# First group of a bidirectional recurrence: low-rank products emitted one direction early, the output gate beside the value projection, one addition moved to ScalarE

## The chip, the cores and the metric

One core of one Trainium2 chip runs the whole program in one launch. The metric is device time in microseconds (us) of that launch, median of several runs. The engines are named as the profile names them: PE (TensorE, matmul), PEld (its weight loads), DVE (VectorE), ACT (ScalarE), POOL (GpSimd), SP (SyncE, which issues most DMAs).

## The reference, cut to what matters

A trunk of four layers over 256 context and 256 latent positions of width 1024: a gated mixer, an RWKV-7 layer (bidirectional), an attention layer, and a gated mixer again. The change touches the RWKV-7 layer only. Its features and its recurrence are

```python
decay = exp(-exp(log_w))             # log_w from w0 + tanh(h w_lora1) w_lora2, per direction n
a     = sigmoid(a0 + (h a_lora1) a_lora2)                                     # per direction n
k_dir = k * (1 + (a - 1) * k_a);  kk = k*k_k / |k*k_k|
for t:  S = S*w_t - (S kk_t)(kk_t a_t)^T + v_t k_t^T;   y_t = S r_t           # both directions
out = (norm(y) + bonus(r, k_dir, v)) * silu(z);   z = (lerped h) w_in[3]
```

There are 16 heads of 64, two directions, 512 positions. The kernel works in chunks of 64 positions, so that the recurrence becomes matmuls and the inverse of triangular 64x64 matrices.

## The kernel before, in words

`rwkv` runs, after the projections r, k, kk and the two low-rank factors (`wl`, `al`) are made, four **groups** of four heads. The steps of a group g are:

- `features(g)`: four **lanes** (two pairs of heads `pr` by two directions `n`). A lane takes two second low-rank products on PE (`pw`, `pa`, lines L715 and L716), a tanh of each on ACT (L730, L735), adds 1 to the first (L731, on POOL), runs a prefix sum on DVE (L739), two exponentials on ACT (L741, L742), and forms the tiles `AR` (L752, L753) and `BK` (L767 on POOL, L768 on DVE). Its inputs k, r, kk come back from DRAM (`fetch`, L720), the weights of the products are loaded by L707 and split in two by a cast (L709) and a subtraction (L711).
- `inverse(g)`: the products `nab` (L789) for the four lanes, copied into `X` (L792, L794), a transposition (L801), 31 steps of substitution on DVE (L806, L807), two transpositions back (L811, L813), and a correction of small products (`pg` L826, `px` L837), which ends in `X`.
- `chain(g)`: eight steps of the recurrence (pz, pu, py, pd and, one step ahead, `operands`: pe, pbk). From the second pu on it needs `X` of its group.
- `gate(g)`: 32 matmuls (L976) for z, with its weights and inputs loaded by L964 and L971, a tanh and a product.

`values()` is not split by groups: for each half c of the columns it makes four blocks of v (L1076, eight matmuls each), a reversed copy of each (`prv`, L1083) written out to DRAM (L1091), and transposed copies (`vfm`, L1096). Its weights `wv` are loaded by L1063, two tiles of 1 MB for each half.

The order of the work is written by hand with `interleave`: each flow is a generator that gives up its turn at every `yield`, and the flows take turns by weights. A scheduler then sets the order on every engine from that; every engine works through its own row in order, and SP too issues its loads in order. Before the change, `values()` runs beside `features(0)` and then `inverse(0)`; in group g, `chain(g)` runs beside `features(g+1)`, `inverse(g+1)`, `gate(g)` and the output of the group before.

All small tiles of `features` share one ring `f` of 7 buffers, and `pw` and `pa` share one PSUM buffer (tag `f`). The pool of these tiles ("scan") is opened where the tiles of the projections before it are closed, so a first write to a tile waits for the last use of what lay at that place.

Of the kernel before, what the change touches and what calls it, by code (L numbers as in the profile page):

```python
# [8 lines left out]
F32 = mybir.dt.float32  # L9
# [89 lines left out]
def body(tc, I, out):  # L99
# [389 lines left out]
    def rwkv(m, tail):  # L489
# [182 lines left out]
        nc.gpsimd.memset(cmask[:, :, 0:1], 0.0)  # L672
        Pt = [st(f"P{i}", [128, 8, 65], 1) for i in range(2)]
# [20 lines left out]
        def seg(t):  # L694
            return t.rearrange("p (s t) -> p s t", s=2)
# [4 lines left out]
        def features(g, f):  # L700
            f["12"] = st("12", [128, 4, 8], 3)
            for pr in range(2):
                o = g * 2 + pr
                w2 = {}
                for nm in "wa":
                    raw = st("f", [128, T], NF)[:, 0:256].rearrange("p (n c) -> p n c", n=2)
                    nc.sync.dma_start(out=raw, in_=I[f"rw_{nm}2"][:, :, o * 128:o * 128 + 128])  # L707
                    whi, wlo = st("w2" + nm, [128, 2, 128], 1, F32R), st("l2" + nm, [128, 128], 1, F32R)
# [3 lines left out]
                    w2[nm] = whi, wlo  # L712

                def second(p, nm, n):
# [3 lines left out]
                def fetch(nm, tag="f", n=NF):  # L718
                    t = st(tag, [128, T], n)
                    nc.sync.dma_start(out=t, in_=spill[nm, o])  # L720
                    return t

                ko, ro, kk = fetch("k"), fetch("r"), fetch("kk")
                kd = []
                for n in range(2):
                    lane = n * 2 + pr
                    pw = ps("pw", "f")
                    second(pw, "w", n)
                    tw = st("f", [128, T], NF)
                    S.activation(rev(tw, n), seg(pw), AF.Tanh, scale=0.5, bias=half[:, n, o:o + 1])  # L730
                    nc.gpsimd.tensor_scalar(tw, tw, 1.0, None, ALU.add)  # L731
                    pa = ps("pa", "f")
                    second(pa, "a", n)
                    ta = st("f", [128, T], NF)
                    S.activation(rev(ta, n), seg(pa), AF.Tanh, scale=0.5, bias=half[:, 2 + n, o:o + 1])  # L735
                    yield
                    c = st("f", [128, T], NF)
                    c8 = c.rearrange("p (c t) -> p c t", c=8)
                    V.tensor_tensor_scan(c, cmask.rearrange("p c t -> p (c t)"), tw, 0.0, ALU.mult, ALU.add)  # L739
                    P = Pt[n]  # L740
                    S.activation(P[:, :, 1:65], c8, AF.Exp, scale=-KAPPA2)  # L741
                    S.activation(c, c, AF.Exp, scale=KAPPA2)  # L742
                    nc.gpsimd.tensor_copy(f["12"][:, lane, :], P[:, :, 64])
                    yield

                    def r4(x):

                        return rev(x, n).rearrange("p s (c t) -> p s c t", c=4)

                    for sg in range(2):  # L750
                        ar = st(f"AR{sg}", [128, 4, 2, 64], 8)
                        V.tensor_tensor(ar[:, :, 0, :], r4(kk)[:, sg], P[:, sg * 4:sg * 4 + 4, 0:64], ALU.mult)  # L752
                        V.tensor_tensor(ar[:, :, 1, :], r4(ro)[:, sg], P[:, sg * 4:sg * 4 + 4, 1:65], ALU.mult)  # L753
                        f["AR"][lane, sg] = ar
                    yield
                    b = tw
                    V.scalar_tensor_tensor(out=seg(b), in0=seg(ta), scalar=1.0, in1=rev(kk, n), op0=ALU.add, op1=ALU.mult)
                    S.activation(ta, ta, AF.Identity, scale=half[:, 4, o:o + 1], bias=kab[:, o:o + 1])
                    yield
                    V.tensor_tensor(seg(ta), seg(ta), rev(ko, n), ALU.mult)  # L760
# [716 lines left out]
```

## Time and profile before

| | |
|---|---|
| median of three runs | 1611.43 us (1610.21 to 1616.43) |
| the profiled execution, whole | 1612.92 us |
| its span, first to last instruction | 1611.1 us |
| PE busy | 1519.5 us, 94% of the span |
| DVE / ACT / POOL busy | 1149.1 / 795.2 / 101.1 us |
| mean clock granted to TensorE | 0.98 |
| the stage of the change (end of the projections to the last inverse) | from 543.6 to 935.8 us of the span |

The profiled execution lies 1.5 us above the median. Its span leaves out 1.8 us around the first and the last instruction. Busy time of PE is a share that all stages make up together; the stage of the change is read in windows of its own.

### The profile page before, as it was taken

The page shows a single profiled execution, that of the slowest core. Times are in us where ns is not written, and L with a number is a line of the kernel's source. Part 1 is how long each engine was busy: PE and PEld are TensorE (multiplying, and loading weights), DVE is VectorE, ACT ScalarE, POOL GpSimd, SP SyncE. Part 2 cuts the span into 40 slices and gives each one's busy share as a digit, 9 for nine tenths or more (in the row PEclk, how much of TensorE's full clock was granted, in tenths as well). Part 3 has the DMA queues.
Part 4 walks back from the last instruction along what each step waited for, and adds up shares of the span by engine and source line. Part 5 has one row for each costly group of instructions (what it writes and reads, how often), then busy time and mean ns, then how long its engine had stood idle before and what let it go on. Part 6 is the DMA issues. An engine that isn't in the chain of part 4 may idle for free.

```text
span 1611.1 us, 29355 instructions
## 1 busy us (share of the span) xinstructions
PE 1519.5 (94%) x11860; PEld 1181.4 (73%) x11860; DVE 1149.1 (71%) x2160; ACT 795.2 (49%) x1434; POOL 101.1 (6%) x135
## 2 busy tenths in 40 slices
PE   5999999999988998999998999799999999989998
PEld 2768888888966644776776777688777777768887
DVE  3769998864898377586887844778766666665876
ACT  4534331223665354345345332569866766356543
POOL 0000000000000132303213000000000000000000
PEclk9999999999999999899999999999999999989999
DMA  9766567742144652532433133134321222265452
GB/s 352 271 246 224 191 218 260 261 153 79 53 144 150 183 164 70 153 96 74 126 99 94 62 100 121 53 118 145 115 74 53 80 85 92 70 233 199 165 183 79
DMA packets 95176, 229.07 MB, mean 142 GB/s; under 512 B 26048, under 2 KB 52160, under 8 KB 80576
## 3 DMA queue, kind: packets, MB, share of 16 engines
q1 hardware_dynamic: 92736, 223.00, 40.8%
q10 hardware_dynamic: 2304, 4.20, 0.7%
q8 instruction: 93, 1.52, 0.4%
q14 instruction: 43, 0.35, 0.1%
HBM read 208.81 MB, written 17.83 MB: 141 GB/s over the span
## 4 chain that ended last, share of the span: by engine, by line
PE 47%; DVE 7%; ACT 5%; issue 1%; POOL 1%; DMA 0%; ACTq 0%; POOLq 0%; DVEq 0%
PE fm L323 5%; PE op L323 4%; PE pg L976 3%; PE fm L324 2%; PE op L1047 2%; PE op L324 2%; PE pz L323 2%; PE pu L323 2%; PE po L1358 2%; PE sc L1376 2%; PE pe L862 2%; PE sc L1377 1%; PE pv L416 1%; PE pv L417 1%; PE pz L324 1%
## 5 line engine op out<-in xcount | busy, mean ns | idle before, releaser
L191 DVE TENSOR_TENSOR lo<-raw,hi 128x2048 fp32r<-128x2048 f32 (+3 forms) x161 | 251.7, 1567 | 108.6 <-ACT hi L190 108.1
L190 ACT CAST hi<-raw 128x2048 fp32r<-128x2048 f32 (+3 forms) x161 | 212.1, 1324 | 226.9 <-PE op L327 40.6
L258 DVE SCALAR_TENSOR_TENSOR junk<-adaw,scb 128x1024 f32<-128x1024 f32 x112 | 136.7, 1221 | 10.0 <-DMA adaw<-in_ada_wT 8.1
L323 PE MATMUL op<-s,hi 128*128 128x512 f32 x256 | 91.6, 400 | 0.0
L415 PE MATMUL pv<-hi,hp 128*128 128x512 f32 x192 | 78.2, 409 | 9.1 <-ACT hi L190 6.0
L416 PE MATMUL pv<-lo,hp 128*128 128x512 f32 x192 | 77.7, 405 | 1.7 <-DVE lo L191 1.7
L323 PE MATMUL fm<-hx,hi 128*128 128x512 f32 x200 | 74.1, 411 | 4.1 <-ACT hx L317 3.8
L417 PE MATMUL pv<-hi,hp 128*128 128x512 f32 x192 | 77.2, 402 | 0.0
L324 PE MATMUL op<-s,lo 128*128 128x256 f32 x256 | 71.1, 280 | 0.0
L976 PE MATMUL pg<-xz,wz 128*128 128x256 f32 x256 | 70.2, 408 | 0.0
L767 POOL TENSOR_TENSOR BK<-f 64x256 f32<-64x256 f32 x64 | 57.3, 895 | 44.4 <-DVE f L760 27.4
L866 DVE TENSOR_TENSOR E<-pe,masks 128x512 f32<-128x512 f32 x64 | 41.5, 682 | 25.5 <-PE pe L862 23.0
L324 PE MATMUL fm<-hx,lo 128*128 128x256 f32 x200 | 56.7, 288 | 2.0 <-DVE lo L191 2.0
L323 PEld LDWEIGHTS op<-s,hi 128*128 128x128 f32 x256 | 48.1, 188 | 12.5 <-issue 1.3
L1076 PE MATMUL pv<-wv,xv 128*128 128x512 f32 x128 | 57.2, 596 | 0.0
L1047 PE MATMUL op<-Y,wo 128*128 128x256 f32 x192 | 55.8, 427 | 1.3 <-DVE xT L1051 1.3
L323 PE MATMUL fm<-cq,hi 128*128 128x512 f32 x144 | 55.7, 422 | 0.0
L976 PEld LDWEIGHTS pg<-xz,wz 128*128 128x128 f32 x256 | 47.0, 197 | 11.5 <-issue 3.8
L415 PEld LDWEIGHTS pv<-hi,hp 128*128 128x128 f32 x192 | 37.7, 197 | 19.4 <-ACT hi L190 6.6
L326 PE MATMUL pu<-hp,hi 128*128 128x512 f32 x128 | 51.1, 400 | 0.0
L327 PE MATMUL pu<-hp,hi 128*128 128x512 f32 x128 | 50.5, 395 | 0.0
L328 PE MATMUL pz<-hp,lo 128*128 128x512 f32 x128 | 50.5, 395 | 0.0
(413 smaller groups left out, 4088.2 us busy)
## 6 DMA issues: line engine op xcount, KB each, us to landing
adaw<-in_ada_wT SPq DMA_DIRECT2D x36, 1024.0 KB, 4.9
raw<-in_sgu_v SPq DMA_DIRECT2D x16, 1024.0 KB, 4.8
raw<-in_sgu_u SPq DMA_DIRECT2D x16, 1024.0 KB, 4.8
raw<-in_sgu_z SPq DMA_DIRECT2D x16, 1024.0 KB, 4.7
raw<-in_sgu_o SPq DMA_DIRECT2D x16, 1024.0 KB, 4.8
adaw<-in_ada_w SPq DMA_DIRECT2D x24, 512.0 KB, 9.6
xz<-xz SPq DMA_DIRECT2D x32, 256.0 KB, 4.2
raw<-in_ml_z SPq DMA_DIRECT2D x16, 512.0 KB, 3.6
```

The lines of the kernel that those rows point to most:

```text
L190: S.copy(hi[:, sl], raw[:, sl])
L191: V.tensor_tensor(lo[:, sl], raw[:, sl], hi[:, sl], ALU.subtract)
L258: V.scalar_tensor_tensor(out=junk, in0=raw[:, f, :], scalar=1.0, in1=scb[:, c, :], op0=ALU.mult, op1=ALU.mult, accum_out=m[:, t * 2 + f, c ...
L323: PE.matmul(p, whi, x, start=start, stop=False)
L324: PE.matmul(p[:, 0:256], wlo, x[:, 0], start=False, stop=stop)
L415: PE.matmul(pv[tb], hs[k][:, 0, sl], whi[:, ws_], start=k == 0, stop=False)
L416: PE.matmul(pv[tb], hs[k][:, 0, sl], wlo[:, ws_], start=False, stop=False)
L417: PE.matmul(pv[tb], hs[k][:, 1, sl], whi[:, ws_], start=False, stop=k == 7)
L767: nc.gpsimd.tensor_tensor(bk[H[h], 2 * h:2 * h + 7:2, :], k4[H[h], sg], c4[H[h], sg], ALU.mult)
L976: PE.matmul(p, ws[k // 4][:, k % 4, pr * 128:pr * 128 + 128], xs[k // 2][:, k % 2, :], start=k == 0, stop=k == 7)
L1047: PE.matmul(p[:, ob], w[:, k, ob, :], y[:, k], start=k == 0, stop=k == 1)
L1076: PE.matmul(p, xv[:, k, tb * 128:tb * 128 + 128], ws[k // 4][:, k % 4, :], start=k == 0, stop=k == 7)
```

## The change

1. In group 0 the order of `features` is written out: the products and the tanh of a lane (`front`) are emitted one direction before the rest of that lane (`back`), and the weights of the second pair (`operand(1)`) at the very start. For that the first group borrows tiles: k, r, kk and the prefix sums go into the spare buffers of `X` and `BK`, the second pair's weights into two of `BK`, and `pa` gets the PSUM buffer with tag `n`. `features` of the groups 1 to 3 keep their order.
2. In all groups the addition of 1 moves from POOL to ACT (an Identity with a bias of one).
3. `gate(0)` no longer runs beside `chain(0)`. It follows `values()`, in the flow that runs beside `features(0)` and `inverse(0)`, and takes the tiles of `wv` for its weights and inputs.
4. `values()` gives up its turn once more, in the middle of each block; its ring `v` has 6 buffers where it had 8. Its first 16 turns run beside `features(0)`, the rest and the gate beside `inverse(0)`.

```diff
+            if g == 0:
+                x = st("X", [128, 32, 64], 2)
+                spare = [x[:, 8 * i:8 * i + 8, :] for i in range(4)] + [st("BK0", [128, 9, 64], 8)[:, 0:8, :] for i in range(4)]
+                spare = [t.rearrange("p u t -> p (u t)") for t in spare]
+                wide = [st("BK1", [128, 9, 64], 8, F32R) for i in range(2)]
+            def fetch(nm, o):
+                t = spare.pop(0) if spare else st("f", [128, T], NF)
+                nc.sync.dma_start(out=t, in_=spill[nm, o])
+                return t
...
-                    nc.gpsimd.tensor_scalar(tw, tw, 1.0, None, ALU.add)
-                    pa = ps("pa", "f")
...
+                S.activation(tw, tw, AF.Identity, bias=one)
+                pa = ps("pa", "f" if g else "n")
...
+                ds = [operand(0)]
+                t0 = front(ds[0], 0)
+                ds.append(operand(1))
+                yield
+                t1 = front(ds[0], 1)
+                yield from back(ds[0], 0, *t0)
+                t0 = front(ds[1], 0)
+                yield from back(ds[0], 1, *t1)
+                total(ds[0])
+                t1 = front(ds[1], 1)
+                yield from back(ds[1], 0, *t0)
+                yield from back(ds[1], 1, *t1)
+                total(ds[1])
...
+                w = vw.tile([128, 8, 256], F32, tag="w", name="wz", bufs=3)
+                    x = vw.tile([128, 8, 256], F32, tag="w", name="xz", bufs=3)
...
+                        if k == 3:
+                            yield
-                    v = vw.tile([128, T], F32, tag="v", name="v", bufs=8)
+                    v = vw.tile([128, T], F32, tag="v", name="v", bufs=6)
...
-        interleave((values(), 20), (chained(features(0, fs[0]), inverse(fs[0])), 50))
+        beside = chained(values(), gate(0, fs[0]))
+        interleave((features(0, fs[0]), 18), (islice(beside, 16), 16))
+        interleave((inverse(fs[0]), 25), (beside, 24))
...
-            steps, ahead, z = chain(g, f), iter(()), gate(g, f)
+            steps, ahead, z = chain(g, f), iter(()), gate(g, f) if g else iter(())
```

What this does to the rows of instructions is shown at three places. The first is SP, where the stage's loads begin, with the semaphores that each load waits for in brackets (DMAHW: an earlier DMA; PE_49: a count of finished PE work). Before:

```order
L683 DMA f<-wl 64x512 [waits DMAHW1_49,DVE_49]
L683 DMA f<-wl 64x512 [waits DMAHW2_49]
L683 DMA f<-al 64x512 [waits DMAHW4_49,PE_49,Activation_49]
L683 DMA f<-al 64x512 [waits DMAHW5_49]
L1063 DMA wv<-in_rw_v 128x2048 [waits DMAHW6_49]
L1063 DMA wv<-in_rw_v 128x2048 [waits DMAHW7_49]
L707 DMA f<-in_rw_w 128x2x128 [waits DMAHW0_49]
```

After (L685 is the old L683, L714 the old L720, L1120 the old L1063, L723 the old L707):

```order
L685 DMA f<-wl 64x512 [waits DMAHW2_49]
L714 DMA X<-k_3339 128x512 [waits DMAHW4_49,PE_49]
L714 DMA X<-r_3628 128x512 [waits DMAHW5_49]
L714 DMA X<-kk_3413 128x512 [waits DMAHW6_49]
L685 DMA f<-al 64x512 [waits DMAHW7_49,Activation_49]
L685 DMA f<-al 64x512 [waits DMAHW0_49]
L1120 DMA wv<-in_rw_v 128x2048 [waits DMAHW1_49]
L1120 DMA wv<-in_rw_v 128x2048 [waits DMAHW3_49,DMAHW2_49,Activation_49]
L723 DMA f<-in_rw_w 128x2x128
```

Three loads into the borrowed `X` now stand ahead of `al` and of the values' weights. In the built program the count that the first of them waits for is that of the last product but one of the r projection's last block (pj, L327); the count that `al` waited for before belonged to an earlier block.

The second place is PE, from the last product of the projection (pj) on. Before:

```order
L328 MATMUL pj<-xs,lo 128x512
L1076 MATMUL pv<-wv,xv 128x512 x8
L715 MATMUL pw<-wx,w2w 128x512
L716 MATMUL pw<-wx,l2w 128x512
L1083 MATMUL prv<-v,flip 128x512
L715 MATMUL pa<-ax,w2a 128x512
L716 MATMUL pa<-ax,l2a 128x512
L1076 MATMUL pv<-wv,xv 128x512 x8
```

After (L1133 is the old L1076, L740 and L741 the old L715 and L716):

```order
L1133 MATMUL pv<-wv,xv 128x512 x2
L740 MATMUL pw<-wx,w2w 128x512
L741 MATMUL pw<-wx,l2w 128x512
L740 MATMUL pa<-ax,w2a 128x512
L1133 MATMUL pv<-wv,xv 128x512
L741 MATMUL pa<-ax,l2a 128x512
L1133 MATMUL pv<-wv,xv 128x512
...
L1133 MATMUL pv<-wv,xv 128x512 x4
```

The first lane's products now follow two products of the values, where eight stood ahead of them, and the second lane's products come before the block's last four.

The third place is PE at the end of the first group's inverse. Before:

```order
L1083 MATMUL prv<-v,flip 128x512
L1076 MATMUL pv<-wv,xv 128x512 x8
L826 MATMUL pg<-Dm,X 32x32 x32
L1096 MATMUL vfm<-ident,v 128x128
L1083 MATMUL prv<-v,flip 128x512
L1096 MATMUL vfm<-ident,v 128x128 x3
L715 MATMUL pa<-ax,w2a 128x512
L716 MATMUL pa<-ax,l2a 128x512
L837 MATMUL px<-X,Tm 32x32 x32
```

After (L1033 is the gate, the old L976; L878 and L889 the old L826 and L837):

```order
L1142 MATMUL prv<-v,flip 128x512
L1155 MATMUL vfm<-ident,v 128x128 x2
L1033 MATMUL pg<-xz,wz 128x256 x4
L1155 MATMUL vfm<-ident,v 128x128 x8
L1033 MATMUL pg<-xz,wz 128x256 x20
L878 MATMUL pg<-Dm,X 32x32 x32
L1033 MATMUL pg<-xz,wz 128x256 x4
L889 MATMUL px<-X,Tm 32x32 x32
L1033 MATMUL pg<-xz,wz 128x256 x4
```

Twenty-four of the gate's 32 products now stand between the last block of values and the first small product that needs the inverse, the other eight between the small products.

## Rows read from the trace of the kernel before

**Rows 1.** The page: busy time, share of the span and instructions of each engine.

```profile
PE 1519.5 (94%) x11860; PEld 1181.4 (73%) x11860; DVE 1149.1 (71%) x2160; ACT 795.2 (49%) x1434; POOL 101.1 (6%) x135
```

**Rows 2.** Busy time of each engine by stage: from:to in us from the span's start, length, busy us and instructions of PE, PEld, DVE, ACT, POOL, then the clock granted to TensorE, the share of the DMA engines and GB/s. The bounds are the start of the values, their second half, the start and end of PE's wait for the first inverse, the first product of the recurrence, and then by turns the start and the end of DVE's work on the inverse of groups 1 and 2.

```profile
543.60:583.50 39.90, 39.46 (x111) 16.77 (x109) 21.68 (x41) 21.01 (x35) 16.30 (x19) 1.00 0.58 163
583.50:624.60 41.10, 39.39 (x332) 19.12 (x331) 35.12 (x76) 16.69 (x36) 12.22 (x13) 1.00 0.40 107
624.60:629.80 5.20, 0.00 (x0) 0.00 (x0) 4.79 (x13) 0.57 (x1) 0.00 (x0) 0.90 0.24 50
629.80:656.60 26.80, 24.00 (x410) 18.57 (x410) 12.81 (x20) 14.23 (x25) 6.75 (x9) 0.70 0.56 169
656.60:691.80 35.20, 31.50 (x601) 25.13 (x602) 20.02 (x43) 15.75 (x37) 11.70 (x13) 0.95 0.40 128
691.80:735.10 43.30, 41.67 (x630) 32.18 (x623) 42.23 (x109) 15.87 (x32) 4.32 (x6) 0.99 0.30 93
735.10:792.20 57.10, 51.99 (x928) 38.68 (x926) 37.01 (x78) 32.61 (x64) 19.86 (x22) 0.97 0.33 99
792.20:836.20 44.00, 42.02 (x616) 31.81 (x616) 42.59 (x110) 16.21 (x32) 1.92 (x2) 1.00 0.31 97
```

**Rows 3.** The order of time on PE, at the start of the values and around the first inverse: start us, us, engine line op out<-in, shape, records (an f32 matmul leaves two), and in brackets the idle time before it with what ended it.

```profile
543.37 0.39 PE L328 MATMUL pj<-xs,lo 128*128 128x512 f32 x1
543.60 7.03 PE L1076 MATMUL pv<-wv,xv 128*128 128x512 f32 x16
550.06 0.79 PE L715 MATMUL pw<-wx,w2w 128*128 128x512 f32 x1
...
592.36 1.08 PE L789 MATMUL nab<-AR,BK 64*32 64x64 f32 x64 [1.61 <-ACT X L794]
...
629.84 1.92 PE L826 MATMUL pg<-Dm,X 32*32 32x32 f32 x64 [5.29 <-DVE Dm L811]
631.95 1.91 PE L1083 MATMUL prv<-v,flip 128*128 128x512 f32 x2
...
643.83 0.74 PE L789 MATMUL nab<-AR,BK 64*32 64x64 f32 x34 [1.45 <-ACT X L841]
653.46 3.26 PE L976 MATMUL pg<-xz,wz 128*128 128x256 f32 x8
660.57 1.99 PE L976 MATMUL pg<-xz,wz 128*128 128x256 f32 x8
```

**Rows 4.** Windows of 2 us, columns as in Rows 2, for the clock granted after PE's wait.

```profile
634.00:636.00 2.00, 2.00 (x31) 1.12 (x31) 0.00 (x0) 1.96 (x5) 0.70 (x1) 0.61 0.00 0
654.00:656.00 2.00, 2.00 (x6) 1.60 (x5) 0.44 (x1) 0.00 (x0) 0.00 (x0) 0.50 1.01 242
```

**Rows 5.** SP's queue around the start of the values (start us, us, line, load), and the wait that held the second low-rank factor there (engine line waited for: us in total, times, longest).

```profile
532.72 1.10 SPq L683 DMA_DIRECT2D f<-al  x2
533.88 3.60 SPq L1063 DMA_DIRECT2D wv<-in_rw_v  x2
545.01 0.65 SPq L707 DMA_DIRECT2D f<-in_rw_w  x1
549.30 0.43 SPq L720 DMA_DIRECT2D f<-kk  x1
SPq L683 <- PE pj L327: 3.8, 1, 3.8
```

**Rows 6.** Issues from 530 to 560 us: load, engine, count, KB each, median us from issue to landing; and, last, the shortest, median and longest landing of all four loads of `wv`.

```profile
wv<-in_rw_v SPq DMA_DIRECT2D x3, 1024.0 KB, 7.3
vt<-v SPq DMA_DIRECT2D x4, 64.0 KB, 6.3
f<-in_rw_w SPq DMA_DIRECT2D x1, 128.0 KB, 2.8
DMA to landing us min/median/max: 5.5/6.9/8.4
```

**Rows 7.** The order of time on ACT and DVE: the weights of the first products, and the first and second inverse.

```profile
547.85 0.40 ACT L709 CAST w2w<-f 128x256 fp32r<-128x256 f32 x1
550.22 0.60 DVE L711 TENSOR_TENSOR l2w<-f,w2w 64x128 fp32r<-64x128 f32 x2
596.85 1.95 DVE L801 STREAM_TRANSPOSE Dm<-X 128x1024 f32<-128x1024 f32 x1 [3.92 <-ACT X L792]
629.69 1.87 DVE L813 STREAM_TRANSPOSE X<-Tm 128x1024 f32<-128x1024 f32 x1
691.78 1.94 DVE L801 STREAM_TRANSPOSE Dm<-X 128x1024 f32<-128x1024 f32 x1 [4.70 <-ACT X L792]
```

**Rows 8.** The addition on POOL (duration ns min/median/max, first and last start), and two operations of ACT with one 128x512 f32 input in SBUF (count, busy us, mean ns, idle before).

```profile
L731 POOL TENSOR_SCALAR f<-f x16: 1489/1491/1583, 552.1 to 874.1; 128x512 f32<-128x512 f32 x16
L758 ACT ACTIVATE f<-f,kab,half 128x512 f32<-128x512 f32 x16 | 12.9, 807 | 7.5 <-DVE f L757 7.5
L742 ACT ACTIVATE f<-f 128x512 f32<-128x512 f32 x16 | 10.0, 624 | 0.4
```

**Rows 9.** The order of time on DVE and POOL while an addition of POOL runs beside the steps of the inverse.

```profile
599.84 0.70 DVE L806 TENSOR_TENSOR tmp<-Dm,Tm 128x87 f32<-128x87 f32 x1
600.57 0.25 DVE L807 TENSOR_TENSOR Tm<-Tm,tmp 128x87 f32<-128x87 f32 x1
599.82 1.49 POOL L731 TENSOR_SCALAR f<-f 128x512 f32<-128x512 f32 x1 [7.68 <-issue]
```

More of the change, by code (lines that the diff above doesn't have):

```diff
@@ L701, in features, with operand @@
             f["12"] = st("12", [128, 4, 8], 3)
-            for pr in range(2):
+            spare, wide = [], []
+            if g == 0:
[7 more added lines that the diff above has]
+                return t
+            def operand(pr):
                 o = g * 2 + pr
@@ new lines, in front, with back, r4 @@
+                S.activation(rev(tw, n), seg(pw), AF.Tanh, scale=0.5, bias=half[:, n, o:o + 1])
+                S.activation(tw, tw, AF.Identity, bias=one)
+                pa = ps("pa", "f" if g else "n")
+                second(pa, "a")
+                ta = st("f", [128, T], NF)
+                S.activation(rev(ta, n), seg(pa), AF.Tanh, scale=0.5, bias=half[:, 2 + n, o:o + 1])
+                return tw, ta
+            def back(d, n, tw, ta):
+                o, lane = d["o"], n * 2 + d["pr"]
+                ko, ro, kk = d["k"], d["r"], d["kk"]
+                c = spare.pop(0) if spare else st("f", [128, T], NF)
+                if g == 0:
+                    spare.append(c)
+                c8 = c.rearrange("p (c t) -> p c t", c=8)
+                V.tensor_tensor_scan(c, cmask.rearrange("p c t -> p (c t)"), tw, 0.0, ALU.mult, ALU.add)
+                P = Pt[n]
+                S.activation(P[:, :, 1:65], c8, AF.Exp, scale=-KAPPA2)
+                S.activation(c, c, AF.Exp, scale=KAPPA2)
+                nc.gpsimd.tensor_copy(f["12"][:, lane, :], P[:, :, 64])
+                yield
+                def r4(x):
+                    return rev(x, n).rearrange("p s (c t) -> p s c t", c=4)
+                for sg in range(2):
+                    ar = st(f"AR{sg}", [128, 4, 2, 64], 8)
+                    V.tensor_tensor(ar[:, :, 0, :], r4(kk)[:, sg], P[:, sg * 4:sg * 4 + 4, 0:64], ALU.mult)
+                    V.tensor_tensor(ar[:, :, 1, :], r4(ro)[:, sg], P[:, sg * 4:sg * 4 + 4, 1:65], ALU.mult)
+                    f["AR"][lane, sg] = ar
+                yield
+                b = tw
+                V.scalar_tensor_tensor(out=seg(b), in0=seg(ta), scalar=1.0, in1=rev(kk, n), op0=ALU.add, op1=ALU.mult)
+                S.activation(ta, ta, AF.Identity, scale=half[:, 4, o:o + 1], bias=kab[:, o:o + 1])
+                yield
+                V.tensor_tensor(seg(ta), seg(ta), rev(ko, n), ALU.mult)
+                d["kd"].append(ta)
+                b4, c4, k4 = (x.rearrange("p (s c t) -> p s c t", s=2, c=4) for x in (b, c, ta))
+                for sg in range(2):
+                    bk = st(f"BK{sg}", [128, 9, 64], 8)
+                    for h in range(2):
+                        nc.gpsimd.tensor_tensor(bk[H[h], 2 * h:2 * h + 7:2, :], k4[H[h], sg], c4[H[h], sg], ALU.mult)
+                    V.scalar_tensor_tensor(out=bk[:, 1:8:2, :], in0=b4[:, sg], scalar=-0.5, in1=c4[:, sg], op0=ALU.mult, op1=ALU.mult)
+                    f["BK"][lane, sg] = bk
+                yield
@@ L776, in features @@
+            for pr in range(2):
+                d = operand(pr)
+                for n in range(2):
+                    t = front(d, n)
+                    yield
+                    yield from back(d, n, *t)
+                total(d)
                 yield
```

100 lines of the change are left out of this document (39 added, 61 removed).

## Prediction, made before the changed kernel ran

> **What bounds the kernel now.** The busy times come first: PE works 94% of the span, DVE 71%, ACT 49%, POOL 6% [rows 1]. That is a mean over the program, so the windows of the stage come next [rows 2]. From 543.6 to 624.6 us PE is busy 39.46 of 39.9 and 39.39 of 41.1 us at a granted clock of 1.00: there PE's amount of work is the time. Then PE stands still for 5.2 us, in which DVE is busy 4.79, and in the next 26.8 us the clock averages 0.70. In the group after that the picture splits. While DVE works on an inverse (691.8 to 735.1) both are full, DVE 42.23 and PE 41.67 of 43.3 us. Between two inverses (735.1 to 792.2) PE has 51.99 of 57.1 and DVE 37.01.
>
> The order of time on PE names the gaps [rows 3]: 5.29 us before the first small product `pg`, ended by DVE's `Dm`, and two of 1.61 and 1.45 us before `nab`, ended by ACT's copy into `X`. What the long gap costs behind it stands in the fine windows [rows 4]: PE is busy all 2.00 us of each, yet the granted clock is 0.61 and 0.50, the lower of the two levels (1.2 GHz). Of the 24.0 us of PE work in the 26.8 us window, 30% was lost to that, 7.2 us [rows 2].
>
> So beside 1.6 + 1.45 us of short waits there is one long wait, worth 5.3 + 7.2 us with what follows. Last I read SP's queue, since loads decide when a stage can begin. Before the change, `al` was issued at 532.7 and the first `wv` at 533.9, ten us before their first product, so PE went from the projection's end to `pv` without a gap [rows 3, 5].
>
> **The change part by part.**
>
> *The gate as cover.* PE's row after the last `nab` runs from about 596.9 (where DVE starts the inverse, [rows 7]) to 624.55, 27.7 us, while DVE has `Dm` ready 33 us after its start (629.84 less 596.85, [rows 3, 7]). By the order, three value products less stand in that stretch (7.03 us for eight, so −2.6, [rows 3]), and 24 gate products and twelve small transposed copies more. A gate product is two records; eight records took 3.26 us at the lower clock and 1.99 behind it [rows 3], so 24 products are 12 us; the copies I put at 1. That is 38 us of PE work against 33: the gap goes and with it the fall of the clock. The two short waits go too, as more PE work stands ahead of them: −8.4 us of waits, −7.2 of clock. If the cover failed, both would come back.
>
> The gate's inputs take the places of `wv`, so the first `xz` can be loaded only from the fourth product before the end of the values. Three and a half us of products, one `prv` (1.91 us at the lower clock [rows 3], so about 1) and the copies lie over its issue and landing. Small loads near a 1 MB load landed after 6.3 us in the median, a quiet one after 2.8 [rows 6]: a wait of 0 to 3 us, taken as +1.
>
> *The start.* In the row of SP, loads of k, r and kk into the borrowed `X` now stand ahead of `al` and both `wv`. The first waits for the last products of the projection, which end near 543.5 [rows 3]; before, `al` waited for an earlier block, and only 3.8 us [rows 5]. Everything behind waits with it: three loads at 0.43 and two at 0.55 put the first `wv` at about 546, and it lands 5.5 to 8.4 us later [rows 5, 6], at 551.5 to 554.4, where its first product stood at 543.60. After two products PE meets `pw`, whose weights are issued behind both `wv` (another 3.6 us, [rows 5], so near 549) and need 2.8 to 6.3 us to land and some 1.1 for the cast and the subtraction [rows 6, 7]: 553 to 556.5. So PE idles 8 to 12 us less the 1.8 us of those two products, and runs some of the next 5 us at the lower clock, as after the gap before. This stage was PE's own, so nothing hides it: +8 to +15, taken as +11.
>
> *The turn order.* The fourth `nab` stands behind three value products (2.6) and one `prv` (1.0) more, less the 1.6 us wait that they fill. With the start, the first inverse begins 11 + 3.6 − 1.6 = 13 us late, near 610.
>
> *Where this leaves PE.* To the second inverse: +11 − 8.4 − 7.2 + 1 = −3.6. But half of the gate, 16 products and 8 us, was done after that inverse's start and now comes before it, and two `pw` (0.9) go behind: the second inverse starts at 691.8 + 3.5, about 695. Those 8 us are missing from PE's row afterwards and come back only where PE sets the pace. Of the 100.4 us to the third inverse that is the 57.1 between inverses; in the other 43.3 DVE is as full [rows 2]. I take that share, 57%, so 4.6 come back (bounds 0 and 8). From the third group on, the orders of both kernels differ only in a lane's place. Net without the lanes: −3.6 + 8 − 4.6 = −0.2.
>
> *The addition.* On POOL it takes 1.49 us, sixteen times [rows 8]. For ACT's Identity on the same tile no row exists; the two nearest with one 128x512 input took 0.62 and 0.81 us [rows 8], I take 0.70: 0.8 saved for each lane. The 11 us on ACT lie in an engine that is half idle. In the lane the addition stands between tanh and prefix sum, so it counts where DVE waits for a lane between two inverses, for one or two of four lanes in each of three groups: 3 to 6 times 0.8, taken as −3.6 (0 to −7). POOL beside DVE also costs: a step of the inverse took 0.70 us beside an addition, where the next, of equal size, took 0.25 [rows 9]; 16 times 0.45 is at most 7 us, most of it where DVE isn't waited for, so nothing is added for it.
>
> The Trainium skill ("SBUF — State Buffer", section "Who interferes with whom") says that a DVE instruction with two SBUF inputs and a GpSimd instruction that reads SBUF exclude each other for the whole instruction. By that rule each addition would block DVE for its full 1.49 us. The row doesn't agree in size: the DVE step started 0.02 us after the addition and was done after 0.70, before the addition's end [rows 9].
>
> Sum: −0.2 − 3.6 = −3.8 against the profiled 1612.9 us gives 1609, and the median lies 1.5 lower: **1608 us**. The bounds that matter are the start (−3 to +4), the gate that is paid back (−3.4 to +4.6) and the lanes (−3.4 to +3.6). The likeliest case's own range is 1601 to 1615.
>
> **Rivals.**
>
> *B, faster: PE is the bound throughout.* For it speaks PE's 94%, and its 52 of 57 us between inverses. Then all 8 us of the gate return, the start costs 8, and the lanes are worth 7: 8 − 8.4 − 7.2 + 0 − 7 = −15, so 1612.9 − 15 − 1.5 = 1597. Against it: in each inverse DVE is as full as PE. The case that the borrowed tiles don't hold the loads up belongs here too; then the start costs nothing, but the semaphores in the order speak against it.
>
> *C, slower: the first inverse's delay is carried on.* Each group's inverse, recurrence and next features form one chain; if that sets the pace, the 13 us by which the first inverse is late are not made up by removed PE waits, and only the lanes' 3.6 come off: 1612.9 + 13 − 3.6 − 1.5 = 1621. It decides if the second inverse starts after 700. For it: both engines full in the inverses, and `X` awaited by the second step of the recurrence. Against it: before the change PE had 24 + 31.5 us of work in the 62 us between, part of it at half clock, which makes slack for a late chain.
>
> *D, DVE freed.* If the addition did block DVE for all of its time, 24 us of DVE would go, of which the inverses and lanes could turn perhaps half into time, beside the −3.8: near 1595. The exclusion that the Trainium skill states on the page named above is this case. One row speaks against it.
>
> **How the numbers follow.** Chances: the forecast 0.48, B 0.29, C 0.20, D 0.03. 0.5% or 8 us is about what a measurement of this kernel can tell from no change, so "same" is 1603.4 to 1619.5: B and D are faster, C slower, the forecast the same. The range takes in B's centre with a little for a cheaper start, and C's centre: 1594 to 1622.
>
> **What would show it.** In the trace after: SP's `al` and `wv` issued after 543.5, the first `pv` after 551 and a clock near 0.5 behind it; no wait of PE before the first inverse's small products, and a clock of 1.00 from 620 to 660; inverses starting near 610 and 695; the addition on ACT at about 0.7 us. The prediction falls if PE starts the values without a gap (then B, or better), if the second inverse starts after 700 (C), or if the gate's loads arrive so late that PE waits before the gate and the clock falls there instead.

## The result, and the profile of the changed kernel

The changed kernel takes 1630.68 us (median of four runs, 1624.32 to 1636.55), the kernel before 1612.82 beside it: ratio 1.0108, 95% interval 1.0059 to 1.0158. It is slower by about 18 us, above the range of 1594 to 1622, where the forecast was 3 us shorter than before. The profiled execution took 1626.96 us, 14.0 more than that of before.

Where the 14 us stand is read from the starts of the four inverses on DVE. Before, they are at 596.85, 691.78, 792.22 [rows 2, 7] and 894.92; after, at 609.74, 702.81, 808.92 and 909.52: +12.9, +11.0, +16.7, +14.6. The loss is there before the first inverse starts, and nothing behind it gives it back. In the profiled execution after, the projection ended at 541.9 us where it ended at 543.8 before, so counted from there the first inverse is late by 14.8 us.

The start of the values, SP's queue and then PE after (start us, us, engine line op; in brackets the idle time before it and what ended it):

```profile
541.70 0.33 SPq L714 DMA_DIRECT2D X<-k  x1
542.55 0.42 SPq L714 DMA_DIRECT2D X<-kk  x1
543.07 1.14 SPq L685 DMA_DIRECT2D f<-al  x2
544.25 3.33 SPq L1120 DMA_DIRECT2D wv<-in_rw_v  x2
...
547.63 0.63 SPq L723 DMA_DIRECT2D f<-in_rw_w  x1
```

```profile
551.33 3.35 PE L1133 MATMUL pv<-wv,xv 128*128 128x512 f32 x4 [9.44 <-DMA wv<-in_rw_v]
554.51 0.50 PE L740 MATMUL pw<-wx,w2w 128*128 128x512 f32 x1
...
608.17 1.08 PE L841 MATMUL nab<-AR,BK 64*32 64x64 f32 x64
...
645.97 4.54 PE L1033 MATMUL pg<-xz,wz 128*128 128x256 f32 x12 [2.10 <-DMA xz<-xz]
650.44 1.20 PE L878 MATMUL pg<-Dm,X 32*32 32x32 f32 x64
...
668.98 1.12 PE L971 MATMUL pu<-Z,X 64*64 64x64 f32 x16
```

Before, `al` left at 532.72 and `wv` at 533.88 [rows 5], and the first product of the values stood at 543.60 without a gap [rows 3]. Now `wv` leaves at 544.25 and PE waits 9.44 us for it. The 5.29 us wait for `Dm` [rows 3] is gone: the gate's products run there until 650.44, after a wait of 2.10 us for `xz`.

DVE after, the end of the first inverse and the second:

```profile
609.74 1.96 DVE L853 STREAM_TRANSPOSE Dm<-X 128x1024 f32<-128x1024 f32 x1 [20.94 <-ACT X L844]
639.99 2.09 DVE L863 STREAM_TRANSPOSE Dm<-Tm 128x1024 f32<-128x1024 f32 x1
702.81 1.94 DVE L853 STREAM_TRANSPOSE Dm<-X 128x1024 f32<-128x1024 f32 x1 [2.84 <-ACT X L844]
750.32 1.87 DVE L865 STREAM_TRANSPOSE X<-Tm 128x1024 f32<-128x1024 f32 x1
```

`Dm` is ready at 642.08, so the small products start 8.4 us after they could. And DVE stood idle for 20.94 us ahead of the first inverse: the features, started 4.5 us later than before, were done early on DVE, and then `nab` waited in PE's row behind products of the values.

The stages after, in windows as in [rows 2]: the gap, what follows it, the first inverse, what follows the wait for `xz`, from the first inverse's end to the second, the second inverse, to the third, the third.

```profile
541.80:551.30 9.50, 0.09 (x1) 0.00 (x1) 2.75 (x4) 4.18 (x7) 0.00 (x0) 0.61 0.93 308
551.00:555.00 4.00, 3.67 (x6) 1.43 (x6) 0.52 (x3) 0.76 (x2) 0.00 (x0) 0.61 1.03 387
609.74:643.89 34.15, 34.12 (x110) 18.94 (x108) 32.29 (x74) 11.39 (x20) 4.58 (x5) 1.00 0.48 124
646.00:650.00 4.00, 4.00 (x11) 3.20 (x12) 0.75 (x2) 0.69 (x3) 0.97 (x2) 0.57 0.17 60
643.89:702.81 58.92, 49.52 (x978) 40.94 (x982) 31.25 (x64) 28.88 (x60) 15.47 (x19) 0.87 0.41 128
702.81:752.19 49.38, 46.86 (x688) 36.49 (x684) 46.81 (x118) 18.52 (x37) 3.19 (x5) 0.92 0.16 50
752.19:808.92 56.73, 52.18 (x882) 37.65 (x880) 34.80 (x71) 32.54 (x63) 14.85 (x19) 0.88 0.31 94
808.92:849.95 41.03, 39.06 (x554) 30.08 (x548) 38.69 (x98) 13.30 (x27) 0.00 (x0) 1.00 0.32 98
```

For the stretch between the first two inverses the row of before that answers is:

```profile
631.56:691.78 60.22, 53.76 (x954) 41.96 (x952) 31.05 (x61) 29.96 (x62) 18.43 (x22) 0.85 0.48 150
```

Beside the first inverse PE now works 34.12 of 34.15 us at a clock of 1.00, as forecast. Right behind it the wait for `xz` is followed by a clock of 0.57, from 646 to 650: the prediction named a wait before the gate with a fall of the clock there as a sign that it falls. From its end to the second inverse the length hardly changes (58.92 and 60.22), though PE has less to do: its idle time grew from 6.5 to 9.4 us and the clock is still 0.87. Of the 9.4 us, 2.1 are the wait for `xz`, and 5.4 are three waits for the recurrence's `S` and `UV`. The second inverse grew from 43.3 to 49.4 us, with 118 instructions of DVE in it for 109 [rows 2] (among the added ones three of `E`, one of `UV` and two of `Y`, all of the recurrence, and three of the output, `xT`); the third shrank from 44.0 to 41.0.

### The profile page after: what moved, and what is told of

Its sections match the earlier page's. It is cut to its first block, busy times and chain, and to the rows that moved or that the text cites. A ratio compares the mean times of both kernels' runs of the same rounds, so it can differ in the third digit from the quotient of the medians.

```text
span 1625.2 us, 29332 instructions
## 1 busy us (share of the span) xinstructions
PE 1528.9 (94%) x11860; PEld 1191.0 (73%) x11860; DVE 1155.1 (71%) x2160; ACT 804.5 (50%) x1450; POOL 79.0 (5%) x120
## 5 line engine op out<-in xcount | busy, mean ns | idle before, releaser
L417 PE MATMUL pv<-hi,hp 128*128 128x512 f32 x192 | 76.8, 400 | 0.0
L1033 PE MATMUL pg<-xz,wz 128*128 128x256 f32 x256 | 67.8, 401 | 2.1 <-DMA xz<-xz 2.1
L1133 PE MATMUL pv<-wv,xv 128*128 128x512 f32 x128 | 59.2, 609 | 9.4 <-DMA wv<-in_rw_v 9.4
L1033 PEld LDWEIGHTS pg<-xz,wz 128*128 128x128 f32 x256 | 46.7, 194 | 12.5 <-issue 2.6
L1133 PEld LDWEIGHTS pv<-wv,xv 128*128 128x128 f32 x128 | 24.2, 194 | 38.0 <-issue 37.4
L327 PE MATMUL pu<-hp,hi 128*128 128x512 f32 x128 | 50.5, 395 | 0.0
```

The source lines that it names most:

```text
L417: PE.matmul(pv[tb], hs[k][:, 1, sl], whi[:, ws_], start=False, stop=k == 7)
L1033: PE.matmul(p, ws[k // 4][:, k % 4, pr * 128:pr * 128 + 128], xs[k // 2][:, k % 2, :], start=k == 0, stop=k == 7)
L1133: PE.matmul(p, xv[:, k, tb * 128:tb * 128 + 128], ws[k // 4][:, k % 4, :], start=k == 0, stop=k == 7)
```

## Experiments

The theories at first: (1) the start is late, and the first inverse's delay is carried through all groups; (2) PE's sum decides, and the gate's cover is worth what was forecast; (3) the gate and the changed turns cost the time, and the start would be made up for. All runs in one table. The columns are the starts of the first, second and fourth inverse and the length of the second, the span of the profiled execution (all us from the traces), then the median of all runs and the ratio to before with its 95% interval. Each ratio is to the kernel before as measured beside that kernel (its medians lie between 1612.4 and 1613.5). A span is that of one execution. In these executions the projection, which no edit touches, ends between 540.5 and 544.6 us, so a start in the table carries up to 2 us either way that no edit made.

| kernel | 1st | 2nd | 2nd's length | 4th | span | median | ratio |
|---|---|---|---|---|---|---|---|
| before | 596.9 | 691.8 | 43.3 | 894.9 | 1611.1 | 1612.8 | |
| changed | 609.7 | 702.8 | 49.4 | 909.5 | 1625.2 | 1630.7 | 1.0059 to 1.0158 |
| S, loads behind `wv` | 608.5 | 705.0 | 49.5 | 910.5 | 1624.5 | 1630.4 | 1.0075 to 1.0115 |
| Gb, gate back | 611.1 | 703.0 | 40.9 | 905.5 | 1619.3 | 1621.2 | 1.0036 to 1.0066 |
| SGb, both | 612.5 | 703.6 | 40.9 | 909.9 | 1624.5 | 1622.2 | 1.0035 to 1.0069 |
| Add alone | 595.2 | 691.9 | 44.0 | 893.5 | 1607.2 | 1605.9 | 0.9933 to 0.9968 |
| SP8 | 601.3 | 697.6 | 49.6 | 900.9 | 1617.3 | 1620.1 | 1.0020 to 1.0080 |
| B1 | 598.7 | 695.5 | 41.2 | 896.6 | 1610.9 | 1614.7 | 0.9998 to 1.0035 |
| G, gate alone | 606.0 | 698.8 | 48.1 | 906.0 | 1620.2 | 1624.9 | 1.0054 to 1.0107 |
| G8, with ring 8 | 599.0 | 692.7 | 48.1 | 897.4 | 1613.5 | 1614.3 | 1.0003 to 1.0042 |
| S8, start mended | 599.6 | 693.8 | 48.1 | 897.3 | 1610.8 | 1614.4 | 0.9994 to 1.0047 |
| B2 | 596.5 | 693.3 | 40.9 | 895.0 | 1608.5 | 1611.4 | 0.9983 to 1.0033 |
| F, feature order | 595.4 | 696.3 | 43.3 | 894.7 | 1608.5 | 1612.7 | 0.9976 to 1.0019 |
| PV | 609.1 | 705.3 | 49.6 | 911.6 | 1625.2 | 1628.3 | 1.0061 to 1.0121 |
| SV | 611.0 | 704.6 | 48.9 | 910.9 | 1627.1 | 1627.7 | 1.0065 to 1.0135 |
| K8 | 592.0 | 693.8 | 44.5 | 893.2 | 1607.2 | 1612.9 | 0.9971 to 1.0017 |
| K5 | 583.4 | 689.3 | 43.8 | 890.7 | 1604.2 | 1611.8 | 0.9967 to 1.0007 |

### The loads behind `wv` (S)

```diff
+                if g == 0:
+                    with tc.issue_after(state["wv"].ins):
+                        nc.sync.dma_start(out=t, in_=spill[nm, o])
```

> The changed kernel with one edit: the group's k, r and kk loads are queued on SP behind the two wv loads. Theory 1 (the late start sets everything: one chain of features, inverse and recurrence carries the first inverse's delay): first pv back at about 543.6 without the 9.4 us gap, but pw still waits for its weights until about 550, so some 4 to 5 us of the gap are left; first inverse at about 604 instead of 609.7, and the whole 5 to 7 us shorter than the changed kernel, about 1624 for a median of 1630.7. Theory 2 (PE's sum): gap and slow clock after it are PE's own, so the same 5 to 7 us. Theory 3 (the gate ahead of the small products and the recurrence's altered turns are the cost, the start is made up later): no change, 1630.

PE in this kernel, at the start:

```profile
540.70 1.88 PE L1137 MATMUL pv<-wv,xv 128*128 128x512 f32 x4
549.49 0.80 PE L744 MATMUL pw<-wx,w2w 128*128 128x512 f32 x1 [6.91 <-ACT w2w L733]
```

The wait for `wv` is gone and another stands there: after two products PE reaches `pw` and waits 6.91 us for its weights. The weights come late because SP's queue was held for 12.0 us at the second load of `wv`, which has a cause of its own (kernel G below). The first inverse came 1.2 us earlier and the time stayed. Read by itself this looked like theory 3; but the start had not been mended, only the name of the wait had changed.

### The gate back (Gb), and both (SGb)

```diff
-        beside = chained(values(), gate(0, fs[0]))
+        beside = values()
-        interleave((inverse(fs[0]), 25), (beside, 24))
+        interleave((inverse(fs[0]), 25), (beside, 16))
-            steps, ahead, z = chain(g, f), iter(()), gate(g, f) if g else iter(())
+            steps, ahead, z = chain(g, f), iter(()), gate(g, f)
```

> The changed kernel with one edit: gate(0) runs beside the first recurrence again, as before the change, with its own tiles; the rest of values beside the inverse. Theory 1 (chain): the small products no longer stand behind the gate's 24 products, so they start when DVE has Dm, near 642 instead of 650.4; second inverse at about 697 to 700 instead of 702.8, second inverse's DVE stretch 43 to 45 us instead of 49.4, so 6 to 10 us shorter than the changed kernel, 1621 to 1625. Theory 2 (PE's sum): PE stands still for about 6 us before the small products and the clock falls behind it, as before the change; the gate no longer covers that, so 5 to 12 us longer, 1636 to 1642.

> Both edits: loads of k, r and kk behind wv, and gate(0) beside the first recurrence. If start and gate are separate costs, the gains add: 11 to 17 us shorter than the changed kernel, 1614 to 1620, close to the kernel before. If one of them hides the other (a later start gives the gate's cover), less than the sum.

PE in Gb, at the first small product and at the recurrence's first `pu`:

```profile
643.40 1.92 PE L878 MATMUL pg<-Dm,X 32*32 32x32 f32 x64 [4.44 <-DVE Dm L863]
...
667.94 0.68 PE L971 MATMUL pu<-Z,X 64*64 64x64 f32 x16
```

Gb is 9 us faster than the changed kernel by the medians. PE waits 4.44 us for `Dm` again, the clock behind it is 0.52 (643.4 to 668.0), and still the second inverse starts where it did, 703.0 for 702.8, and the first `pu` 1 us sooner than in the changed kernel: the wait that the gate covered was worth nothing there. The second inverse is 40.9 us long. SGb gains nothing over Gb, as S itself gained nothing, and misses its expectation of 1614 to 1620.

### The addition alone (Add)

```diff
-                    nc.gpsimd.tensor_scalar(tw, tw, 1.0, None, ALU.add)
+                    S.activation(tw, tw, AF.Identity, bias=one)
```

> The kernel before with the addition of 1 moved from POOL to ACT and nothing else. The prediction's term: 0.7 us on ACT for 1.49 on POOL, 3 to 7 us shorter in all, 1606 to 1610 for a median of 1612.8. Rival (the lane is not waited for, or ACT's queue holds the addition up as long as POOL did): no change within 2 us. Rival of the blocked DVE: 12 us or more shorter.

ACT's row for it, grouped (count, busy us, mean ns, idle before):

```profile
L733 ACT ACTIVATE f<-f,one 128x512 f32<-128x512 f32 x16 | 11.5, 722 | 0.4
```

0.72 us for POOL's 1.49 [rows 8]. The span is 3.9 us shorter, the median 7.7, interval of the ratio 0.9933 to 0.9968. The expectation gave two ways to a gain, the shorter lane and a DVE that POOL no longer slows; which of them brought it, no run separates. This is the one kernel whose interval lies wholly below 1, and it is faster than both the kernel before and the changed one.

### The start mended further (SP8, B1)

```diff
+        interleave(islice(beside, 2))
-        interleave((features(0, fs[0]), 18), (islice(beside, 16), 16))
+        interleave((features(0, fs[0]), 18), (islice(beside, 14), 14))
```

SP8 is S with these lines: eight products of the values stand ahead of the first `pw`, as before the change. B1 has also the gate back, and the four turns of `nab` in one piece:

```diff
+        inv = inverse(fs[0])
+        interleave(islice(inv, 5))
+        interleave((inv, 20), (beside, 16))
```

> The changed kernel with the start mended in both its parts: k, r and kk are loaded behind wv, and the first block of values (eight products) stands ahead of the first pw, so that nothing waits for the weights of pw. Gate and turns as in the changed kernel. Theory 1 (chain: the first inverse's delay is carried through the groups): no gap at 541 to 551, first inverse near 597 to 599, 10 to 13 us shorter than the changed kernel, 1618 to 1621. Theory 3 (the gate and the fuller second inverse set the time, the start is absorbed before the second inverse): first inverse near 598, but second inverse still near 702 and no change, 1628 to 1631.

> The changed kernel with the start mended, the gate beside the first recurrence again, and the four nab turns of the first inverse taken without value turns between. Theory 1: first inverse near 596, second near 690, 20 to 24 us shorter than the changed kernel, 1607 to 1611, that is as the kernel before with its addition on ACT. Theory 3: as with the gate back alone, 1621, since the start is absorbed.

SP8 gains 10 us, and the first inverse is at 601.3. So theory 3 falls in its claim that the start is made up for. B1, at 1614.7, falls short of the 1607 to 1611 expected of it. One wait is left there in PE's row of SP8:

```profile
548.10 5.40 PE L1137 MATMUL pv<-wv,xv 128*128 128x512 f32 x8 [4.17 <-DMA wv<-in_rw_v]
```

### The gate alone (G), and with the ring at 8 (G8)

```diff
-        interleave((values(), 20), (chained(features(0, fs[0]), inverse(fs[0])), 50))
+        interleave((chained(values(), gate(0, fs[0])), 27), (chained(features(0, fs[0]), inverse(fs[0])), 50))
```

The gate takes the tiles of `wv` as in the change; in G the ring `v` has 6 buffers, in G8 it keeps 8.

> The kernel before with the gate of the first group moved behind the values as in the change (tiles of wv, six buffers of v), and nothing else. The prediction's step (the gate covers PE's wait for the first inverse, worth 8 to 15 us at the second inverse, half of the moved work returning later): no wait of 5 us before the small products, clock 1.00 from 625 to 660, 1600 to 1608. Theory 3 (the gate ahead of the small products holds the inverse's end up and the second inverse's DVE stretch grows from 43 to 49 us): 1617 to 1624 for a median of 1613.

> The kernel before with the gate moved as in the change, but with the ring v left at 8 buffers: with 6 the second wv load waited 12 us for r's last store, which had its place, and PE stood still for 4.2 us. This is the gate alone without that wait. If the gate's own cost is the second inverse's longer DVE stretch (48 us where the kernels with the gate beside the recurrence have 41 to 44): first inverse near 597, second inverse's stretch 47 to 50 us, third's 41, 2 to 6 us slower than before, 1615 to 1619. If the wait for wv was all of the loss: first inverse near 597 and no change or faster, 1605 to 1613.

G has the wait for `wv` too, without any loads into `X`. SP's waits from 528 to 556 us in G name it (engine line, what it waited for: us, times, longest):

```profile
SPq L1068 <- DMA r<-ev: 12.0, 1, 12.0
```

The second `wv` load waits for a store of r from the tile `ev`. Before the change such a store held it for 2.7 us only, and the load of `in_rw_w` behind it for 7.5. As the wait of 12.0 us goes with the ring of 6 and is gone with 8, the smaller ring seems to move the pool so that `wv` gets the place of a tile that is stored later; the addresses themselves were not read. G8, at 8 buffers, starts at 542.37 without a wait, and G's 12 us become 2. In G8 the gate didn't cover the wait: PE still waited 4.23 us for `Dm` (4.82 in G), as three quarters of the gate's products stood behind the first small product. So G and G8 price the gate's move and not its cover. The second inverse is 48.1 us long:

```profile
692.74:740.80 48.06, 45.57 (x682) 35.54 (x670) 47.11 (x118) 17.07 (x35) 6.50 (x7) 0.93 0.17 51
```

The same 118 instructions of DVE as in the changed kernel. All kernels with the gate moved have 48 to 50 us here and about 41 in the third; with the gate beside the recurrence it is 41 to 44.5 and 44.

### All three causes of the start mended (S8), with the gate back (B2), and the feature order alone (F)

S8 is SP8 with the ring at 8; B2 is B1 with the ring at 8. F is B2 with the old turns instead of those of B1:

```diff
-                        if k == 3:
-                            yield
...
+        interleave((beside, 20), (chained(features(0, fs[0]), inverse(fs[0])), 50))
```

> The changed kernel with all of its start mended: k, r and kk behind wv, the first block of values ahead of pw, ring v at 8 buffers. Gate and turns as in the change. No wait of PE before 555; first inverse 4 to 6 us earlier than with the ring of 6 (601.3), near 596. If the first inverse's start is carried through: 3 to 6 us shorter than that kernel's 1620, 1614 to 1617. If the gate holds the time: 1620 again.

> As the one before with the gate beside the first recurrence again and the four nab turns together. First inverse near 593 to 595, second inverse's stretch 41 us. If start and gate are the two costs and the new order of the features is worth something: 3 to 6 us shorter than with the ring of 6 (1614.7) and below the kernel with the addition alone (1605.9), 1602 to 1608. If the new order is worth nothing: about that kernel's 1606 to 1610.

> Feature order and addition of the change with the turns of the kernel before (values 20 to 50, no turn within a block, ring of 8), loads of k, r, kk behind wv, gate beside the first recurrence. It differs from the kernel with the addition alone by the order of the first group's features only. If products one direction early shorten the first inverse's way: first inverse at 590 to 593, and 2 to 6 us shorter than 1606. If PE paces the first inverse anyway: no change, 1606.

S8, with gate, order and turns of the change but its start mended, is 16 us faster than the changed kernel and within the noise of before: nearly the whole loss lies in the start. But S8 didn't bring the gain that the forecast had for the gate, and its clock shows a part of the reason (windows as above; the last is the whole stretch between the first two inverses):

```profile
633.72:660.00 26.28, 24.13 (x483) 20.01 (x483) 11.87 (x25) 13.00 (x23) 7.72 (x9) 1.00 0.47 144
664.00:668.00 4.00, 4.00 (x58) 2.84 (x60) 1.63 (x2) 2.84 (x6) 0.00 (x0) 0.50 0.59 194
672.00:676.00 4.00, 4.00 (x44) 2.98 (x40) 1.59 (x4) 1.70 (x3) 0.00 (x0) 0.50 0.14 37
633.72:693.84 60.12, 52.63 (x990) 43.22 (x992) 31.12 (x65) 29.17 (x60) 16.07 (x19) 0.80 0.39 121
```

Up to 660 the clock is 1.00, where before it averaged 0.70 [rows 2]. Then PE waits 1.66 us for the recurrence's state `S`, and behind it the clock is at the lower level, 0.50. The fall was put off, not removed: over the whole stretch the clock is 0.80, where before it was 0.85. B2 and F are as fast as before, though both hold the addition on ACT, and both lie above what was expected of them. Their intervals don't overlap that of the addition alone, so the new order seems to take back what the addition gives. With the order come its borrowed tiles and the other PSUM buffer of `pa`, and no run separates the three. The traces show where the difference stands. PE in F, and in the kernel with the addition alone:

```profile
541.45 7.03 PE L1128 MATMUL pv<-wv,xv 128*128 128x512 f32 x16
562.22 1.12 PE L1135 MATMUL prv<-v,flip 128*128 128x512 f32 x2 [1.12 <-ACT v L1130]
574.51 2.05 PE L1135 MATMUL prv<-v,flip 128*128 128x512 f32 x2 [2.04 <-ACT v L1130]
```

```profile
544.39 7.03 PE L1078 MATMUL pv<-wv,xv 128*128 128x512 f32 x16
```

From the first product of the values to the first inverse F takes 53.9 us and the addition alone 50.8; the 3.1 us between them are about F's two waits of PE for ACT's copies of `v`. From the first inverse's end to the second F takes 66.9 us, the addition alone 62.8.

### One cause of the start at a time (PV, SV)

PV has the block of values ahead of `pw` and the ring at 8, but the loads into `X` ahead of `wv`. SV has the loads behind `wv` and the ring at 8, but only two products ahead of `pw`. Their edits are those of SP8 and S with `bufs=8` for `v`.

> The changed kernel with two of the three mends of the start (first block of values ahead of pw, ring v at 8), so that the loads of k, r and kk ahead of al and wv are the only cause left at the start. If the prediction's term for these loads is right in size: first pv near 551 with a gap of 9 to 10 us, first inverse 8 to 11 us later than with all three mended (599.6), near 608 to 611, and about 1624 to 1627 against 1614.4. If it is the wait for pw's weights that mattered: first inverse near 600 and 1615.

> The changed kernel with the other two mends (k, r, kk behind wv, ring v at 8): the first pw still stands behind two products of the values, so its wait for its weights is the only cause left. Gap of 4 to 6 us before pw near 549, first inverse 4 to 6 us later than with all mended, 1619 to 1622. If the wait is absorbed: 1615.

PE in PV, and in SV:

```profile
551.32 5.46 PE L1133 MATMUL pv<-wv,xv 128*128 128x512 f32 x6 [9.31 <-DMA wv<-in_rw_v]
```

```profile
543.79 1.88 PE L1137 MATMUL pv<-wv,xv 128*128 128x512 f32 x4
548.51 0.79 PE L744 MATMUL pw<-wx,w2w 128*128 128x512 f32 x1 [2.84 <-ACT w2w L733]
550.74 0.79 PE L745 MATMUL pw<-wx,l2w 64*128 64x512 f32 x1 [1.44 <-DVE l2w L735]
```

Either cause alone costs almost all of it: 14 and 13 us over S8's 1614.4. The third alone, the ring (SP8), costs 6. The sum would be 33; together they cost 16. They overlap, which is why taking away the first alone gave nothing. PV came to 1628.3, just above its expectation. SV cost more than its expectation; its two waits at the start are 4.3 us, and two waits of 2.1 and 2.2 us for ACT's copies of `v` follow at 574 and 585. What the rest of the 13 us is, no run shows.

### Fewer values ahead of the first inverse (K8, K5)

B2 with ten turns of the values, and with seven, beside the features instead of sixteen (two of them ahead, `a` is 8 and 5):

```diff
-        interleave((features(0, fs[0]), 18), (islice(beside, 14), 14))
+        interleave((features(0, fs[0]), 18), (islice(beside, a), a))
-        interleave((inv, 20), (beside, 16))
+        interleave((inv, 20), (beside, 30 - a))
```

> Start fully mended, gate beside the first recurrence, addition on ACT, nab turns together, and only ten turns of values beside features(0) instead of sixteen: 32 of the 64 value products stand ahead of the last nab, where it was 38. If the first inverse's start is carried one to one to the last (as read from the twelve kernels before): first inverse near 590 to 592, fourth 4 to 6 us earlier than the kernel before, 1603 to 1608. If PE's work ahead of the recurrence is the bound by then: first inverse early, but recurrence and second inverse no earlier, 1611.

> As the one before with seven turns of values beside features(0): 25 products ahead of the last nab. One to one: first inverse near 586 to 588, 1598 to 1604. PE bound: PE without a wait from 600 to the first recurrence, recurrence near 655 to 658 whatever the inverse's start, and 1608 to 1612. A loss is possible if PE stands still during the features and runs at the lower clock behind it.

The first inverse starts 5 and 13 us earlier than before, the second 2 us later and 2.5 earlier, and the time is that of before. A late first inverse is carried to the fourth in every kernel here (least in Gb, 10.6 of 14.3 us), an early one isn't in full: the stretch to the second inverse grows, to 67.5 us in K8 and 76.8 in K5.

```profile
612.51:689.31 76.80, 69.89 (x1006) 48.62 (x1005) 34.94 (x72) 37.90 (x75) 17.75 (x24) 0.92 0.44 132
```

In K5 PE works 69.89 of those 76.80 us, where before it had 53.76 of 60.22: the values that no longer stand ahead of the inverse stand behind it. And the first `pu` stands at 655.9 in K5 and at 659.8 in K8, for 657.9 before, however early the inverse was. So it is likely PE's work up to the second inverse that a delay at the start adds to. That is theory 2 for the start, and it fits what theory 1 only describes; it isn't shown in full, as PE wasn't without a wait there (in K5 it worked 53.0 of the 60 us from 600 to 660).

## Why the prediction was wrong

**The start** was read rightly in its first effect: loads into `X` ahead, first product at 551.33 (forecast 551.5 to 554.4), a clock of 0.61 behind it. The first inverse at 609.74 (forecast 610) is partly luck: counted from the end of the projection it came 14.8 us late where the working has 13, and the projection ended 1.9 us sooner in that execution. The start was charged 11 us; the mended S8 shows 16 by the medians and 14 by the spans (1625.2 less 1610.8). The queue's price alone, PV against S8, is 14. The working had also missed a cause, the ring's: the order shows more semaphores on the second load of `wv` than before, and they were passed over.

**The failed step is the gate's cover**, −8.4 us of waits and −7.2 of clock, carried to a second inverse at 695. The wait for `Dm` did go and the clock was 1.00 beside the first inverse, but the second inverse started at 702.81. From the first inverse's start to the second's took 93.1 us, where the forecast had 85 (610 to 695) and the kernel before 94.9. The pair that differs in the gate alone says it most plainly: Gb, with a wait of 4.44 us and the low clock behind it, takes 91.9. S8 against B2, which differ in the gate and in the turns of `nab`, have 94.2 and 96.8; there the first `pu` did come 5.8 us sooner behind the first inverse, and 2.6 of that were left at the second. Two things were overlooked. All 32 products of the gate now stood ahead of the recurrence, and they took what the wait had cost: they held the small products up for 8.4 us longer than DVE needed, and the first `pu` came 59.2 us after the first inverse's start, for 61.0 before and 56.8 in Gb. The row of before for that `pu` is:

```profile
657.89 0.68 PE L919 MATMUL pu<-Z,X 64*64 64x64 f32 x16
```

And PE's waits and low clock, gone in one place, were back in the next: for `xz`, priced at +1 us with no clock lost, and for the recurrence's `S` and `UV`; 9.4 us idle in the stretch that had 6.5. (The 6.3 us that the working took as the landing of small loads is that of `vt<-v` [rows 6], which are stores.)

**The work that was to be paid back** was guessed at 4.6 of 8 us, which puts the third inverse 95.8 us behind the second. It took 106.1, for 100.4 before. In the eight kernels with the gate moved it is 103.1 to 106.1, in the others 97.6 to 100.7. The second inverse got longer by 5 to 6 us than before and the third shorter by 3, in each kernel with the gate moved: with the gate gone from PE's row, the order put more of the recurrence's DVE steps among the steps of the inverse (118 instructions for 109). By G8 the gate's move as a whole costs 2 us (interval of the ratio 1.0003 to 1.0042), by S8 against B2 3, and in the kernels with a late start 8 to 9 (the changed kernel against Gb, S against SGb). In the sum the moved gate stood with a gain of 11 (−8.4 − 7.2 + 1 + 8 − 4.6).

**The addition** was right in sign and in its duration (0.72 for an estimated 0.70); its worth, −3.6, is −3.9 by the spans and −7.7 by the medians, just past its bound of −7. The case in which DVE is freed of a whole block, 24 us, didn't come. **The new order of the features**, which the sum put at nothing beyond the start, costs about 7 us by the medians of F and of the addition alone.

Put together by the medians, the start's 16, the gate's 2, the addition's −8 and the order's 7 give +17 for a measured +18; the forecast had 11, −11, −4 and 0. The parts come from different kernels and do interact, so the agreement is partly luck.

**The rivals.** C had the right sign, its condition (second inverse after 700: 702.8) and, at the fourth inverse, its price (+13 for a measured +14.6); its whole time, 1621, was short of 1630.7 by what it took off for the lanes and by the spread between the profiled execution and the median. It had 0.20. Its mechanism, a chain of inverses that sets the pace, is only half borne out: a late first inverse was carried on, but an early one (K8, K5) was not. The argument against C, slack in PE's row, was the mistake: idle time and low clock remained, 9.4 us and 0.87 for 6.5 and 0.85, and 5.4 of the 9.4 us were waits inside the recurrence.

## What to carry to other kernels

When a change borrows buffers or makes a ring smaller, look at the semaphores of every load that now stands at the head of its queue, and at the loads behind it: each of the three causes here put a wait in front of an engine that had been 99% busy [rows 2]. When one cause is undone and nothing happens, read the trace before dropping the theory; the next wait may have taken its name. A covered wait is worth something only if what it fed starts earlier, so forecast that start and not the wait.

## What the runs showed of the hardware

The length of a single wait of PE didn't tell whether the clock falls behind it. In S8 one of 1.66 us at 661.75 was followed by a clock of 0.50 from 664 on, in the changed kernel one of 2.10 us by 0.57 (646 to 650). Before the change a wait of 1.61 us at 592 was followed by no fall (clock 1.00 from 583.5 to 624.6, [rows 2]), and in SV one of 2.11 us at 574.18 by none (1.00 from 574 to 580), though one of 2.24 us at 585.19 was (0.50 from 586 to 588). What the two kinds differ in, no run here was made to tell. An Identity on ACT from a 128x512 f32 tile in SBUF took 0.72 us. In the kernel before, four steps of the inverse on DVE took 0.81 to 0.83 us beside POOL's products into `BK` (616.95 to 620.3), where steps of the same shapes took 0.40 to 0.42; three others beside the same products, at 615.17 to 616.50, took 0.41.
